# A recorded single-core trunk layer: RWKV inverses in place through one scratch tensor, scores in pieces, ACT-issued stores, new prices in the recorder

## The chip, the cores and the metric

The kernel runs on one core of one Trainium2 chip. Its time is the device time in microseconds (us) of one execution. The engines of the core are PE (matrix products into PSUM banks), DVE, ACT and POOL (elementwise work; POOL cannot read PSUM) and SP, which here only issues DMA transfers. Each engine works through its own instructions in the order in which the program holds them, and waits when an operand is not there yet.

## The reference, cut to what matters

One layer of a hybrid encoder reads 1024 prompt tokens and 64 sample tokens through one wide input projection and feeds three token mixers: RWKV-7 (A), mLSTM (B) and stick-breaking attention (C). Their outputs are gated, projected, merged and projected again. The change is in mixer A, whose state goes through the tokens one by one:

```python
def step(S, inp):
    r_t, w_t, k_t, v_t, kk_t, a_t = inp
    sa = jnp.einsum('bhvk,bhk->bhv', S, -kk_t)
    S = (S * w_t[:, :, None, :] + sa[..., None] * (kk_t * a_t)[:, :, None, :]
         + v_t[..., None] * k_t[:, :, None, :])
    return S, jnp.einsum('bhvk,bhk->bhv', S, r_t)
```

The kernel takes 64 tokens (a chunk) at a time. Inside a chunk the recurrence is a triangular system, so each chunk of each of the 8 heads needs the inverse of a 64 x 64 unit triangular matrix, before the chain over the chunks can use it.

## The kernel before, in words

**Two strands.** `main` is the strand of projections. Its 78 blocks of the input projection each take 72 products: 8 slices of the contraction, three products for each slice (high and low parts of a float32r split, lines 755 on), and three groups of 384, 384 and 320 tokens. That is 5616 products whose operands are called `xh` or `xl` and `whl`. After them come the merges (operands `heapr` and `whl` first), and then the tail (output projection, layer norm, last gates). `side` is the strand of the mixers: A for four pairs of heads, each in two halves of 8 and 9 chunks, then B for four heads, then C for four pairs of heads, and then `m_prep`, which loads, multiplies and splits the first operand of the merges. The merges wait for it (`m_begin`, and `merge` by `self.ycd`).

**What sets the order.** All work is recorded while the program is built. `Sched` keeps a clock for each engine, and every helper (`mm`, `act`, `tt`, `scan`, `dma` ...) hands it a price. After each projection product, `poll` looks at the waiting side tasks and records those whose operands are ready by these clocks. So between a side product and the one that needs its result stand as many projection products as the prices say will fill the time. When the projections run out, the side products stand alone. The profile attributes work to the helpers' lines: L321 is every product, L328 every transpose, L353 ACT, L358 and L376 DVE, L360 POOL, L427 a DMA.

**Mixer A for one half of a pair.** `a_front` loads the projected columns from DRAM and prepares them; its part "scores" makes two masked 128 x 128 matrices for each chunk (buffer `SC`) and stores the 32 x 32 diagonal blocks of the first one to the DRAM tensor `nd` with 8 DMAs. `a_inverse` loads them with one block in a partition, and inverts all blocks of the half at once on POOL, in 31 steps of two instructions, from `N` into a second buffer `Q` that begins as the identity. DVE copies a transposed form, and two DRAM tensors, `qd` and `xd`, take the results. `a_corner` loads both with 10 DMAs, then completes the 64 x 64 inverses with products of 32 x 32 on PE. `a_chain` follows the chunks with three dependent steps of PE and ACT or DVE for each chunk. Inverses follow one another on POOL; the chain of one half, the inverse of the next and the front of a third run beside each other.

**Stores.** The blocks of projections for B, C and the gates leave through four staging buffers. `store` spawns a task that issues the DMA on SP, in whose queue it waits until ACT or DVE has written the buffer.

Of the kernel before, what the change touches and what calls it, by code (L numbers as in the profile page):

```python
# [9 lines left out]
F32 = mybir.dt.float32  # L10
# [3 lines left out]
OP = mybir.AluOpType  # L14
# [10 lines left out]
HEAP = 17256  # L25
# [281 lines left out]
class K:  # L307
# [75 lines left out]

    def rsqrt(self, y, x, h, eps):
# [440 lines left out]
    def raw(self, i, col, dst, kind, done):  # L825
# [8 lines left out]
        def ev(g, t0, n, bank):  # L834
# [10 lines left out]
            self.store(i_, dst[:, t0:t0 + n], d, done if g == 2 else None)  # L845
# [4 lines left out]
    def store(self, i, out, d, done):  # L850

        self.kept |= {i}
# [457 lines left out]
    def a_all(self):  # L1310
# [5 lines left out]
        inv = [self.must(n, True) for n in (1024, 1024, 256, 288)]  # L1316
        self.bkd = self.must(1024, True)
        lists = ("Z", "ya", "bn")
        self.ast = [*Z, *cst["ya"], *cst["bn"], *[x for k, x in cst.items() if k not in lists], *inv, self.bkd]
# [12 lines left out]
    def a_front(self, p, hf):  # L1332
# [93 lines left out]
        SC = yield from self.get(nc * 256)  # L1426
        UV = yield from self.get(nc * 128)
        sc4, uv3 = SC.v(nc, 2, 128), UV.v(nc, 128)
        bd5 = self.bkd.v(2, 2, 2, 128)

# [10 lines left out]
        for c0 in range(0, nc, 4):  # L1441
            cr = range(c0, min(c0 + 4, nc))
            m = len(cr)
            bs = [(yield from self.bank()), (yield from self.bank())]
# [26 lines left out]
            for i in range(min(m, 2)):  # L1471
                w = (m + 1 - i) // 2
                yield self.act(uv3[64:128, c0 + i:c0 + m:2, :], b2[64 * i:64 * i + 64, :w * 128].rearrange(
# [738 lines left out]
```

## Time and profile before

| | |
|---|---|
| runs | 1891.88 us median of 3 (1881.05 to 1899.76) |
| profiled execution | 1887.65 us, its span 1885.9 us |
| mean granted PE clock | 0.973 of full speed |
| busy share of the span | DVE 62%, ACT 42%, POOL 30%; PE's share is with the rows below |
| DMA | mean 110 GB/s, 207338 of 212280 packets in the queue of SP |

Busy PE time counts products that overlap in the array, so a share near 100% means that PE did not run dry, and not that it was at its peak. The granted clock has two levels, 2.4 GHz (1.0) and 1.2 GHz; a stretch's value is a mean. An idle engine costs time only where PE, which has the most work, waits for it.

### The profile page before, as it was taken

To read this page: it belongs to the slowest core of one execution; us is meant where nothing else is said; L and a number is where in the kernel's file an instruction comes from. 1 tells how busy PE (TensorE), PEld (TensorE's weight loads), DVE (VectorE), ACT (ScalarE), POOL (GpSimd) and SP (SyncE) were. 2 spreads that over 40 slices of the span, in tenths; PEclk is the share of its full clock that TensorE was granted. 3 is DMA by queue.
4 is the path that set the end of the run, shared out by engine and by line. 5 is a ranking of instruction groups with operands and counts; after the bars stand their busy time and mean duration, and the time that the engine had idled before them with its cause. 6 is when DMAs were issued, how large, how long until landed. Compare 5 with 4: busy or idle time off the path is not lost.

```text
span 1885.9 us, 30250 instructions
## 1 busy us (share of the span) xinstructions
PE 1763.8 (94%) x10873; PEld 1619.1 (86%) x10873; DVE 1178.7 (62%) x2588; ACT 784.9 (42%) x1781; POOL 556.9 (30%) x1028
## 2 busy tenths in 40 slices
PE   6999999989999999999999999999966799988999
PEld 5999888979898899999999999999844799866787
DVE  8346466564647554756876266666666678888643
ACT  5444444344444344545444354645453222211321
POOL 6007445362617522810611221212020000345100
PEclk9999999999999999999999999999977899989999
DMA  4323423223232332343633442423211877522321
GB/s 148 109 83 87 112 71 95 80 83 109 77 92 67 110 85 77 99 119 114 198 122 115 141 125 68 116 90 110 72 53 35 264 229 232 158 90 78 125 80 60
DMA packets 212280, 206.55 MB, mean 110 GB/s; under 512 B 41592, under 2 KB 180650, under 8 KB 212130
## 3 DMA queue, kind: packets, MB, share of 16 engines
q1 hardware_dynamic: 207338, 191.86, 33.4%
q0 software_dynamic: 4704, 12.71, 2.1%
q8 instruction: 86, 1.41, 0.3%
q14 instruction: 64, 0.52, 0.1%
q10 hardware_dynamic: 88, 0.04, 0.0%
HBM read 136.25 MB, written 68.34 MB: 108 GB/s over the span
## 4 chain that ended last, share of the span: by engine, by line
PE 41%; issue 8%; DVE 8%; ACT 2%; POOL 2%; DMA 1%; SPq 0%; POOLq 0%; DVEq 0%; ACTq 0%
PE bk L321 39%; PE bk L328 3%; DVE heap L376 2%; DVE heap L397 2%; DVE heap L358 2%; DVE heapr L358 1%; POOL heap L414 1%; ACT heapr L353 1%; ACT heap L353 1%; DMA heap<-yz 1%; DMA heap<-gd 0%; DVE whl L358 0%; DVE heap L408 0%; POOL heap L419 0%; ACT whl L353 0%
## 5 line engine op out<-in xcount | busy, mean ns | idle before, releaser
L321 PE MATMUL bk<-xh,whl 128*128 128x384 f32 (+3 forms) x3792 | 1065.9, 342 | 0.3 <-DVE heap L376 0.3
L321 PEld LDWEIGHTS bk<-xh,whl 128*128 128x128 f32 (+1 forms) x3792 | 685.0, 188 | 11.9 <-issue 3.0
L321 PE MATMUL bk<-xl,whl 128*128 128x384 f32 (+3 forms) x2184 | 674.7, 330 | 1.7 <-POOL xl L360 1.2
L321 PEld LDWEIGHTS bk<-xl,whl 128*128 128x128 f32 (+1 forms) x2184 | 406.0, 189 | 6.0 <-POOL xl L360 1.8
L353 ACT ACTIVATE heap<-bk 64x64 f32<-64x64 f32 (+10 forms) x639 | 216.4, 346 | 433.1 <-PE bk L321 143.9
L360 POOL TENSOR_TENSOR heap<-heap 32x31 f32<-32x31 f32 (+33 forms) x514 | 347.0, 675 | 159.4 <-DMA heap<-nd 121.2
L328 PE MATMUL bk<-ident,heap 128*128 128x128 f32 (+3 forms) x942 | 184.7, 293 | 57.1 <-DVE heap L376 18.5
L358 DVE TENSOR_TENSOR whl<-heap,whl 128x1024 fp32r<-128x1024 f32 (+1 forms) x114 | 122.8, 1078 | 147.8 <-ACT whl L353 121.8
L328 PEld LDWEIGHTS bk<-ident,heap 128*128 128x128 f32 (+3 forms) x942 | 125.3, 149 | 82.3 <-DVE heap L376 21.4
L358 DVE TENSOR_TENSOR heap<-heap 128x256 f32<-128x256 f32 (+18 forms) x376 | 186.4, 501 | 13.6 <-DMA heap<-yz 2.8
L321 PE MATMUL bk<-heap,heap 128*128 128x128 f32 (+3 forms) x1360 | 170.6, 255 | 18.7 <-ACT heap L353 16.6
L321 PEld LDWEIGHTS bk<-heap,heap 128*128 128x128 f32 (+2 forms) x1360 | 142.9, 162 | 46.2 <-ACT heap L353 31.6
L353 ACT ACTIVATE heap<-bk,pc 128x384 f32<-128x384 f32 (+5 forms) x218 | 114.3, 547 | 137.4 <-PE bk L321 102.0
L321 PE MATMUL bk<-heapr 128*128 128x256 f32 (+2 forms) x524 | 131.0, 355 | 12.1 <-DVE heapr L358 5.6
L376 DVE SCALAR_TENSOR_TENSOR heap<-heap 128x4 f32<-128x4 f32 (+9 forms) x265 | 106.0, 402 | 50.4 <-ACT heap L353 45.0
L321 PE MATMUL bk<-heapr,whl 128*128 128x384 f32 (+2 forms) x648 | 119.6, 343 | 18.8 <-ACT heapr L353 18.5
L353 ACT ACTIVATE heap<-heap 64x64 f32<-64x64 f32 (+9 forms) x328 | 111.0, 343 | 61.5 <-DVE heap L376 20.1
L353 ACT ACTIVATE whl<-heap 128x1024 fp32r<-128x1024 f32 (+1 forms) x116 | 105.4, 910 | 68.0 <-PE bk L321 58.9
L321 PEld LDWEIGHTS bk<-heapr,whl 128*128 128x128 f32 x648 | 110.6, 192 | 25.2 <-ACT heapr L353 20.3
L321 PEld LDWEIGHTS bk<-heapr 128*128 128x128 f32 x524 | 89.4, 202 | 29.8 <-DVE heapr L358 12.1
L397 DVE TENSOR_TENSOR_SCAN heap<-heap,cst 128x128 f32<-128x128 f32 (+8 forms) x68 | 96.3, 1420 | 28.2 <-POOL heap L414 16.2
L353 ACT ACTIVATE heap<-bk,hb 128x384 f32<-128x384 f32 (+1 forms) x120 | 67.5, 563 | 109.5 <-PE bk L321 88.9
(153 smaller groups left out, 1808.4 us busy)
## 6 DMA issues: line engine op xcount, KB each, us to landing
heap<-in_w_in_dram SPq DMA_DIRECT2D x77, 512.0 KB
heap<-gt SPq DMA_DIRECT2D x24, 544.0 KB
gt<-heap SPq DMA_DIRECT2D x48, 192.0 KB
heap<-in_x_prompt_dram SPq DMA_DIRECT2D x16, 512.0 KB
heap<-crd SPq DMA_DIRECT2D x12, 544.0 KB
heap<-yd SPq DMA_DIRECT2D x24, 272.0 KB
heap<-yz SPq DMA_DIRECT2D x24, 272.0 KB
heap<-in_w_branch_dram SPq DMA_DIRECT2D x24, 256.0 KB
```

Source lines behind the costliest of these rows:

```text
L321: lambda: self.nc.tensor.matmul(out, lhsT, rhs, start=start, stop=stop, skip_group_check=more),
L328: lambda: self.nc.tensor.transpose(out, in_, self.ident[:p, :p]), load=(0.82 * fsize(in_), d))
L353: return self.nc.scalar.activation(out, in_, func, **kw)
L358: lambda: self.nc.vector.tensor_tensor(out=out, in0=a, in1=b, op=op))
L360: lambda: self.nc.gpsimd.tensor_tensor(out=out, in0=a, in1=b, op=op))
L376: lambda: self.nc.vector.scalar_tensor_tensor(out=out, in0=a, scalar=s, in1=b, op0=op0, op1=op1))
L397: return self.S.emit("dve", fsize(out) * 1.06 + 65, rd, [out], lambda: self.nc.vector.tensor_tensor_scan(out=out, data0=d0, data1=d1, init ...
L414: return self.S.emit("pool", fsize(out) * 1.0 + 130, [in_], [out], lambda: self.nc.gpsimd.affine_select(out=out, in_=in_, pattern=pattern, ...
```

## The change: what it does

**Prices.** A float32r product of n columns costs 13 + n/2.4 ns in the recorder, 1 + n/2.4 before (line 316). A scan on DVE costs 2.13 ns for each element and 90, before 1.06 and 65.

**Inverses.** The masked first score matrix gets its sign from a second mask (`maskb`), so the inverse adds where it subtracted, in 30 steps, in place in `N`. There is no `Q`, no `qd` and no `xd`. `nd` holds whole 64 x 64 blocks; the scores go there with one or two DMAs for every four chunks, as soon as these are made. Blocks of 32 x 32 are loaded from it, inverted and stored back to it, now by rows of 32 numbers; the corner loads 64 x 64 blocks and transposes one half of each on DVE (`tr32`).

**Scores in pieces.** `SC` and `UV` are buffers for four chunks each, freed by the chain after every four chunks.

**Stores.** The stores of the blocks for B, C, the mLSTM's output gate and the merge gates are issued by ACT, behind the ACT instruction that writes the staging buffer: 156 DMAs. Those of kind `z`, which DVE writes, and A's stay with SP.

```diff
-            c = d = 1 + (213.0 if n < 256 else n / 2.4)
+            c = d = 13 + (213.0 if n < 256 else n / 2.4)
...
+    def tr32(self, out, in_):
+
+        return self.S.emit("dve", fsize(out) * 1.06 + 65, [in_], [out], lambda: self.nc.vector.transpose(out, in_))
...
-        return self.S.emit("dve", fsize(out) * 1.06 + 65, rd, [out], lambda: self.nc.vector.tensor_tensor_scan(
+        return self.S.emit("dve", fsize(out) * 2.13 + 90, rd, [out], lambda: self.nc.vector.tensor_tensor_scan(
...
-            self.store(i_, dst[:, t0:t0 + n], d, done if g == 2 else None)
+            self.store(i_, dst[:, t0:t0 + n], d, done if g == 2 else None, kind != "z")
...
-    def store(self, i, out, d, done):
-
+    def store(self, i, out, d, done, now=False):
+
+        if now:
+            self.dma(out, d, "a")
+            if done:
+                self.have.add(done)
+            return
...
-        inv = [self.must(n, True) for n in (1024, 1024, 256, 288)]
+        inv = [self.must(n, True) for n in (1024, 240, 288)]
...
-                yield self.stt(sc4[:, c, 0, :], bs[0][:, i * 128:(i + 1) * 128], nsb[:, c:c + 1],
-                               self.mask[:, c % 2 * 64:c % 2 * 64 + 128], OP.mult, OP.mult)
+                yield self.stt(sc4[:, i, 0, :], bs[0][:, i * 128:(i + 1) * 128], nsb[:, c:c + 1],
+                               self.maskb[:, c % 2 * 64:c % 2 * 64 + 128], OP.mult, OP.mult)
             for e in range(min(m, 2)):
-                yield self.tt(sc4[:, c0 + e:c0 + m:2, 1, :],
+                yield self.dma(nd[c0 + e:c0 + m:2].rearrange("c h s j -> (h s) c j"),
+                               sc4[:, e::2, 0, 64 - 64 * e:128 - 64 * e], "s")
...
-        nd = self.dr.tile([2, 18, 32, 32], F32, name="nd", bufs=3)
-        for k in range(2):
-            for h in range(2):
-                s = slice(64 * h + 32 * k, 64 * h + 32 * k + 32)
-                for e in range(2):
-                    o = 64 - 64 * e + 32 * k
-                    yield self.dma(nd[k, h * nc + e:(h + 1) * nc:2].rearrange("c s j -> s c j"),
-                                   sc4[s, e::2, 0, o:o + 32], "s")
...
+        blk = [nd.rearrange("c h s j -> (c h) s j")[0:B, 32 * k:32 * k + 32, 32 * k:32 * k + 32] for k in range(2)]
+        rows = [N[k * B:(k + 1) * B, :1024].rearrange("p (s j) -> p s j", j=32) for k in range(2)]
         for k in range(2):
...
-        for j in range(31, 0, -1):
-            w = 32 - j
+            yield self.dma(rows[k], blk[k], "s")
+        yield self.memset(N[0:P, :1024][:, ::33], 1.0)
+        yield
+        n3 = N[0:P, :1024].rearrange("p (s j) -> p s j", j=32)
+        for j in range(30, 0, -1):
+            w = 31 - j
...
-                    q3[:, j:j + 1, j:32].to_broadcast([P, j, w]), OP.mult, IE)
-            yield self.tt(q3[:, 0:j, j:32], q3[:, 0:j, j:32], t3, OP.subtract, IE)
+                    n3[:, j:j + 1, j + 1:32].to_broadcast([P, j, w]), OP.mult, IE)
+            yield self.tt(n3[:, 0:j, j + 1:32], n3[:, 0:j, j + 1:32], t3, OP.add, IE)
...
-            yield self.dma(qd[k, 0:B].rearrange("c s j -> c (s j)"), Q[k * B:(k + 1) * B, :1024], "s")
-        yield self.dma(xd[0:B].rearrange("c s j -> c (s j)"), N[0:B, :1024], "s")
+            yield self.dma(blk[k], rows[k], "s")
...
+        for v, cs in parts:
+            yield self.tr32(x13[:, cs, :], v[:, :, 0:32])
...
+                    self.free(SC[c // 4], UV[c // 4])
```

**Where instructions move.** PE holds the same 9887 products and transposes in both programs. Their order differs from the first halves of A on. Counted in the two orders: ahead of the first product of A's fronts (its second operand is the constant `bd`) stand 396 projection products before and 357 now; ahead of the last 32 x 32 product of A's corners 3471 and 2346; between the recording of the first and last product of the eight chains of A stand 1691 projection products and 451 others before, 1295 and 610 now.

PE, where the input projections end (`xh`/`xl`, `whl`), mixer C (`heapr` alone, transposes through `ident`) and the merges (`heapr,whl`) meet. Before, the last projection product is the third row, and 168 rows of C stand between it and the first merge:

```order
L321 MATMUL bk_67<-xh,whl 128x320
L321 MATMUL bk_67<-xl,whl 128x320
L321 MATMUL bk_67<-xh,whl 128x320
L328 MATMUL bk_70<-ident,heap 128x128 x3
L321 MATMUL bk_72<-heapr 128x256 x2
L321 MATMUL bk_68<-heapr 128x256
...
L321 MATMUL bk_68<-heapr 128x256 x3
L321 MATMUL bk_72<-heapr 128x256 x4
L321 MATMUL bk_65<-heapr,whl 128x384 x12
L321 MATMUL bk_66<-heapr,whl 128x384 x12
```

Now the merges follow the last projection product at once; C's last product stands some 540 products further ahead:

```order
L321 MATMUL bk_67<-xl,whl 128x320
L321 MATMUL bk_67<-xh,whl 128x320 x2
L321 MATMUL bk_67<-xl,whl 128x320
L321 MATMUL bk_67<-xh,whl 128x320
L321 MATMUL bk_65<-heapr,whl 128x384 x12
L321 MATMUL bk_66<-heapr,whl 128x384 x12
```

All C products have moved ahead, between projections; behind this place the order of the merges is the same.

SP's queue at the second half of A, where the scores of one half are stored while the inverse of the first half comes back. Before (`nd` and `qd` in slices of 32 partitions, `xsd` the projections for A):

```order
L427 DMA nd<-heap_76 32x5x32
L427 DMA xsd<-heap 128x384
L427 DMA nd<-heap_76 32x4x32
L427 DMA nd<-heap_76 32x5x32
L743 DMA heap<-in_w_in_dram 128x8x128
L427 DMA nd<-heap_76 32x4x32
```

Now (64 x 64 pieces from all partitions, `nd<-heap 16x32x32` is the inverse going back):

```order
L431 DMA nd<-heap_76 128x2x64
L431 DMA xsd<-heap 128x384
L431 DMA nd<-heap_76 128x2x64
L431 DMA xsd<-heap 128x384
L747 DMA heap<-in_w_in_dram 128x8x128
L431 DMA nd<-heap_76 128x2x64
```

SP holds 648 instructions now, 884 before: 156 stores have gone to ACT, and each half of A has 13 of these DMAs where it had 23.

## Rows read from the trace of the kernel before

**Rows 1.** The profile's page: the span, the busy times, the busy tenths of PE in 40 slices of 47.1 us, and the granted clock in tenths.

```profile
span 1885.9 us, 30250 instructions
PE 1763.8 (94%) x10873; PEld 1619.1 (86%) x10873; DVE 1178.7 (62%) x2588; ACT 784.9 (42%) x1781; POOL 556.9 (30%) x1028
...
PE   6999999989999999999999999999966799988999
...
PEclk9999999999999999999999999999977899989999
```

**Rows 2.** Busy time of each engine by stretch. Columns: stretch, length, busy us and (records) of PE, weight loads, DVE, ACT, POOL, then granted clock, DMA share, GB/s. The stretches are the fronts and inverses of A, the rest of A with B, C beside projections, C alone with the preparation of the merges, the merges, the tail.

```profile
97.10:821.40 724.30, 697.40 (x4760) 650.81 (x4758) 412.87 (x1177) 318.73 (x834) 332.69 (x600) 0.99 0.32 91
821.40:1097.60 276.20, 273.67 (x1774) 262.98 (x1767) 172.98 (x489) 129.90 (x317) 63.28 (x129) 1.00 0.43 135
1097.60:1360.50 262.90, 256.20 (x1650) 240.40 (x1649) 179.11 (x204) 136.14 (x261) 46.70 (x152) 1.00 0.31 94
1360.50:1477.10 116.60, 69.72 (x323) 52.65 (x321) 74.19 (x91) 49.49 (x94) 13.83 (x45) 0.75 0.22 67
1477.10:1626.00 148.90, 148.88 (x883) 147.69 (x884) 112.72 (x205) 37.36 (x67) 3.37 (x6) 0.99 0.74 241
1626.00:1885.90 259.90, 236.13 (x1022) 188.08 (x1021) 169.26 (x297) 64.64 (x118) 65.17 (x36) 0.95 0.27 87
```

**Rows 3.** PE in order of time (start, length, operation, count, idle time before it and what ended that): the last projection product and the first merges.

```profile
1360.50 0.31 PE L321 MATMUL bk<-xh,whl 128*128 128x320 f32 x1
...
1451.89 0.62 PE L321 MATMUL bk<-heapr 128*128 128x256 f32 x3 [0.34 <-DVE heapr L358]
1459.30 1.77 PE L321 MATMUL bk<-heapr,whl 128*128 128x384 f32 x3 [6.79 <-ACT heapr L353]
1464.86 1.77 PE L321 MATMUL bk<-heapr,whl 128*128 128x384 f32 x3 [3.79 <-ACT heapr L353]
1470.61 1.76 PE L321 MATMUL bk<-heapr,whl 128*128 128x384 f32 x3 [3.98 <-ACT heapr L353]
1476.36 5.88 PE L321 MATMUL bk<-heapr,whl 128*128 128x384 f32 x23 [3.98 <-ACT heapr L353]
```

**Rows 4.** PE groups by line and tile in the stretch 1360.5 to 1477.1 (count after the x, busy us, mean ns of one, idle time before them).

```profile
L321 PE MATMUL bk<-heapr 128*128 128x256 f32 (+2 forms) x152 | 46.2, 406 | 10.4 <-ACT heapr L353 5.0 <-DVE heapr L358 4.1 <-DVE heap L358 0.5
L328 PE MATMUL bk<-ident,heap 128*128 128x128 f32 (+1 forms) x134 | 29.6, 343 | 17.6 <-DVE heapr L358 10.6 <-DVE heap L358 6.3 <-ACT heap L353 0.7
L321 PE MATMUL bk<-heap 128*128 128x128 f32 (+3 forms) x24 | 6.9, 379 | 0.0
L321 PE MATMUL bk<-heapr,whl 128*128 128x384 f32 x10 | 5.8, 639 | 18.8 <-ACT heapr L353 18.5
```

**Rows 5.** The same groups in 1100 to 1300, where C stands between projections.

```profile
L321 PE MATMUL bk<-xh,whl 128*128 128x384 f32 (+1 forms) x481 | 136.6, 338 | 0.0
L321 PE MATMUL bk<-xl,whl 128*128 128x384 f32 (+1 forms) x241 | 79.2, 329 | 0.0
L321 PE MATMUL bk<-heapr 128*128 128x256 f32 (+2 forms) x260 | 58.6, 328 | 0.7 <-DVE heapr L358 0.5
L328 PE MATMUL bk<-ident,heap 128*128 128x128 f32 (+1 forms) x230 | 41.0, 274 | 4.0 <-DVE heap L358 3.9
L321 PE MATMUL bk<-heap 128*128 128x128 f32 (+3 forms) x48 | 11.5, 330 | 0.0
```

**Rows 6.** The stretch 1500 to 1600 of the merges, columns as in rows 2.

```profile
1500.00:1600.00 100.00, 100.00 (x604) 100.00 (x603) 76.01 (x140) 23.57 (x42) 1.12 (x2) 1.00 0.71 232
```

**Rows 7.** PE groups of projection products in A's stretch, 97 to 821.4.

```profile
L321 PE MATMUL bk<-xh,whl 128*128 128x384 f32 (+3 forms) x2051 | 581.8, 344 | 0.0
L321 PE MATMUL bk<-xl,whl 128*128 128x384 f32 (+2 forms) x1025 | 338.2, 330 | 0.0
```

**Rows 8.** Who waited for whom (total us, times, longest us): products and weight loads of PE in 97.1 to 821.4.

```profile
PE bk L321 <- ACT heap L353: 17.6, 21, 2.2
...
PEld bk L321 <- ACT heap L353: 37.7, 64, 2.4
```

**Rows 9.** Three of the eight inverses on POOL, from first to last instruction (the first, the sixth, the last), columns as in rows 2.

```profile
146.80:188.30 41.50, 40.39 (x255) 38.89 (x254) 28.26 (x58) 18.66 (x47) 36.99 (x70) 1.00 0.23 66
...
564.50:606.50 42.00, 38.25 (x232) 34.70 (x231) 33.35 (x106) 20.06 (x56) 37.26 (x64) 0.96 0.20 60
...
741.20:794.10 52.90, 51.74 (x319) 51.08 (x319) 35.63 (x76) 25.72 (x48) 47.66 (x67) 1.00 0.30 88
```

**Rows 10.** Waits of the whole span (total us, times, longest us): POOL's for the loads of the inverses.

```profile
POOL heap L360 <- DMA heap<-nd: 121.2, 8, 24.7
```

**Rows 11.** The DMAs that ACT issues (shortest, median, longest ns), by the tile they write, and the waits of SP's queue.

```profile
L427 ACTq DMA_DIRECT2D grd<-heap x6: 246/250/271, 208.6 to 217.9; - x6
...
SPq L427 <- ACT heap L353: 583.9, 166, 11.6
```

**Rows 12.** Waits of PE in the merges and the tail, 1480 to 1886.

```profile
PE bk L328 <- DVE heap L376: 18.5, 5, 5.9
```

**Rows 13.** DMAs from POOL's queue (count, KB each, median us from issue to landing).

```profile
out_c_p_dram<-heap POOLq DMA_DIRECT2D x4, 64.0 KB, 2.2
```

More of the change, by code (lines that the diff above doesn't have):

```diff
@@ L24 @@
 COL_CQ, COL_CK, COL_CV, COL_CZ, COL_G = 4744, 5256, 5768, 6280, 6792
-HEAP = 17256
+HEAP = 17264
 SW = 12928
@@ L1315, in a_all @@
                "V2": self.must(128, True), "U2": self.must(128, True), "bn": [self.must(256, True) for _ in range(2)]}
-        inv = [self.must(n, True) for n in (1024, 1024, 256, 288)]
+        inv = [self.must(n, True) for n in (1024, 240, 288)]
         self.bkd = self.must(1024, True)
+        mb = self.must(192, True)
+        self.maskb = mb[:, :192]
+        yield self.cp(self.maskb, self.mask[:, :])
+        yield self.ts(self.maskb[:, 64:128], self.mask[:, 64:128], -1.0, OP.mult)
         lists = ("Z", "ya", "bn")
-        self.ast = [*Z, *cst["ya"], *cst["bn"], *[x for k, x in cst.items() if k not in lists], *inv, self.bkd]
+        self.ast = [*Z, *cst["ya"], *cst["bn"], *[x for k, x in cst.items() if k not in lists], *inv, self.bkd, mb]
         self.bond = self.dr.tile([4, 128, NT], F32, name="bond")
@@ L1425, in a_front @@
         self.S.note(f"   scores {p}{hf}")
-        SC = yield from self.get(nc * 256)
-        UV = yield from self.get(nc * 128)
-        sc4, uv3 = SC.v(nc, 2, 128), UV.v(nc, 128)
+        SC, UV = [], []
         bd5 = self.bkd.v(2, 2, 2, 128)
+        nd = self.dr.tile([9, 2, 64, 64], F32, name="nd", bufs=3)
         def diag(i):
@@ L1443, in a_front @@
             m = len(cr)
+            SC.append((yield from self.get(m * 256)))
+            UV.append((yield from self.get(m * 128)))
+            sc4, uv3 = SC[-1].v(m, 2, 128), UV[-1].v(m, 128)
             bs = [(yield from self.bank()), (yield from self.bank())]
@@ L1552, in a_corner @@
             for h in range(2):
-                yield self.mm(bs[h][top[h], c * 32:(c + 1) * 32], x13[low[h], c, :], sc4[low[h], c, 0, 96 - c % 2 * 64:128 - c % 2 * 64], True, True)
+                yield self.mm(bs[h][top[h], c * 32:(c + 1) * 32], x13[low[h], c, :], tri(c)[low[h], 32:64], True, True)
         for h in range(2):
-            for e in range(2):
-                yield self.act(sc4[top[h], e::2, 0, 96 - 64 * e:128 - 64 * e],
-                               bs[h][top[h], :nc * 32].rearrange("p (a b) -> p a b", b=32)[:, e::2, :], AF.Copy, scale=-1.0)
+            for v, cs in parts:
+                yield self.act(v[top[h], :, 32:64],
+                               bs[h][top[h], :nc * 32].rearrange("p (a b) -> p a b", b=32)[:, cs, :], AF.Copy)
             self.unbank(bs[h])
@@ L1599, in a_chain @@
             C0, nc_ = (0, 8) if hf == 0 else (8, 9)
-            bk3, kr3, sc4, uv3 = BK.v(nc_, 128), KR.v(nc_, 128), SC.v(nc_, 2, 128), UV.v(nc_, 128)
+            bk3, kr3 = BK.v(nc_, 128), KR.v(nc_, 128)
             for c in range(nc_):
+                sc3, uv2 = (x[c // 4].v(min(4, nc_ - c // 4 * 4), n, 128)[:, c % 4] for x, n in ((SC, 2), (UV, 1)))
+                uv2 = uv2[:, 0, :]
                 if c + C0 == 16:
@@ L1626, in a_chain @@
                 u = cb[:, 128:256]
[L1627 to L1628 removed]
+                yield self.mm(u, sc3[:, 0, :], R1[:, :], True, True)
+                yield self.ts(uv2[0:64, :], u[kr, :], -1.0, OP.mult)
                 for h in range(2):
@@ L1637, in a_chain @@
                     yield self.stt(zn[r, r], zz[r, r], PC[r, c:c + 1], ZP[r, r], OP.mult, OP.add)
-                yield self.mm(ry, sc4[:, c, 0, :], U2[:, :], False, True, more=True)
+                yield self.mm(ry, sc3[:, 0, :], U2[:, :], False, True, more=True)
                 zi ^= 1
@@ L1647, in a_chain @@
                     yb = None
-            self.free(BK, KR, PC, SC, UV)
+            self.free(BK, KR, PC)
             self.S.note(f"      chained {p}{hf}")
```

50 lines of the change are left out of this document (21 added, 29 removed).

## The prediction

> **What bounds the kernel now.** I read the page first. PE is busy for 94% of the span, yet its digits fall to 6 in three slices, the only ones after the start in which the granted clock falls below 8 [rows 1]. So the question is whether PE works through one fixed pile of products without a hole. The busy times by stretch answer it [rows 2]: from 97 to 1360 us and in the merges PE is nearly full, and one stretch, 1360.5 to 1477.1, has 69.7 us of work in 116.6 us, at a mean clock of 0.75. PE in order of time tells what happens there [rows 3]: at 1360.50 the last projection product runs, and from then on only C's last head pair and the preparation of the merges are left, with nothing to put between their steps. The first merges come in threes, each after a wait of 4 to 7 us for ACT, which waits for loads. PE is the bound in all other stretches; there the side strand costs only its own products, as long as they come when their operands are ready.
>
> **The exposed stretch, the largest term.** The order now puts 541 products, nearly all of the projections, between C's last product and the first merge. What does C's work cost when it stands between projections? In the merges 604 products take 100 us, 165.6 ns each [rows 6]; these have the same 384 and 320 columns as the projections. In 1100 to 1300, 481 + 241 = 722 projection products take 722 x 0.1656 = 119.6 us, so the 260 + 230 + 48 = 538 products of C, waits included, take the other 80.4 us: 0.150 us each [rows 5]. The exposed stretch holds 152 + 134 + 24 = 310 such products, and 13 of projections and merges (323 in all) [rows 2, 4]. At these prices it would take 310 x 0.150 + 13 x 0.166 = 48.7 us, and 116.6 - 48.7 = **67.9 us go**. Ends: its busy time at its clock, 69.72 x 0.75 = 52 us, would save 64; A's cheaper price (below), 0.128 us, would save 75. The preparation of the merges (the waits at 1459 to 1476) is hidden if it ends within the 541 products, 541 x 0.166 = 90 us; before it took from 1452 to 1477, so it fits. This needs no PE instruction to become faster: the pile is the same 9887.
>
> **A runs with less between its steps.** Of the 3076 projection products in A's stretch [rows 7], 1086 move behind it (counted in the orders, 3471 - 396 stand between the first product of A's fronts and the last of its corners before, 2346 - 357 = 1989 now). At 0.1656 us A's stretch shrinks by 180 us to 544 us, which is no gain by itself, since these products run later. The rest of the stretch, 724.3 - 3076 x 0.1656 = 214.9 us, is for 4760 - 3076 = 1684 records of A's own (0.128 us each, waits included) [rows 2, 7]. Waits are in it already: ACT held up products 21 times and weight loads 64 times, 55.3 us [rows 8]. In the chains, 204 steps of PE (4 pairs, 17 chunks, 3 steps), 1691 projections and 451 others stand between steps before, 1295 and 610 now. An other one costs 214.9 us over the 935 products that the order has for these records (the trace counts most of A's twice), 0.230 us. So a step had (1691 x 0.1656 + 451 x 0.230)/204 = 1.88 us of cover, and has 1.74. If every step used all of its cover, 204 x 0.14 = 29 us of waits come in; if none did, 0. Less than half of the steps wait now (85 events), and half is what I take: **+15**. B has the same kind of chain, but nearly no waits in its stretch, where PE is busy 273.67 of 276.20 us [rows 2]: 0.
>
> **Inverses.** The work of the 30 steps is the sum of j(31 - j), 4960 elements a partition, before 5456; at 36.99 us busy in 41.5 [rows 9] an inverse becomes some 4 us shorter, and the memset of `Q`, the copy and the extra loads go. POOL and the DMA queue are beside PE, so the direct gain is 0; the cover that hides an inverse, from its loads to its corner, is 73 to 88 us of products in the new order at the prices above, and it needs 41.5 us, a load of 15 us on the mean and 24.7 at most [rows 10] and the way back. If it fails, the DVE transposes of the corner wait for DMA, with the splits of weights queued behind them.
>
> **ACT-issued stores.** 156 DMAs at 250 ns [rows 11] are 39 us more on ACT, which is busy for 634 of the 1380 us from 97 to 1477 (four stretches summed [rows 2]); ACT has room, and each DMA stands behind the write it needs, so it waits for nothing. SP's queue loses its 583.9 us of waits for ACT [rows 11], and what stood behind them (loads for A, weights) is issued earlier. Both at 0; ends -10 and +10, an estimate, a quarter of those 39 us either way. Scan prices change only when scans are expected to end: with the first term.
>
> **Merges and tail.** The merges' PE order is unchanged: 0. In the tail three of the nine groups of transposes stand 15 to 24 products earlier. There PE waits for DVE, 18.5 us in 5 events [rows 12]; DVE needs the same time either way, and a wait that begins earlier mostly ends at the same moment. **+3**, ends 0 and 14.
>
> **Sum.** 1887.65 - 67.9 + 15 + 3 = 1837.8 by the profiled execution. That execution lies 4.2 us below the median of the three runs, so 1842 on the median's scale; I say **1840**. Own range of this case: 1887.65 - 75 - 10 = 1803 to 1887.65 - 64 + 29 + 10 + 14 = 1877.
>
> **Rival 1, slower: the inverses cannot follow.** A's half now gets 544/8 = 68 us where it had 90.5. The inverses form a loop on one buffer: load, POOL, store, next load. If that loop needs more than 68 us, PE waits for the difference eight times, and from 68 + 68/8 = 76.5 us on the whole first term is eaten. The last inverse took 52.9 us, beside the gates of B on DVE, the others 40 to 43 of own time; with the longest load wait, 24.7 us, and a store of 2.2 us as POOL's small ones took [rows 9, 10, 13], the loop is 79.8 us. Eight times 11.8 is 94 us: 1887.65 - 67.9 + 94 + 18 = **1932**. For it: DVE's 413 us in A would fill 76% of 544 us, not 57%. Against it: the sixth inverse ran beside a DVE busy for 33.35 of 42.00 us and took 42.0, and the load waits hold the time until the scores were made. The Trainium skill ("SBUF — State Buffer", "Who interferes with whom") states that a DVE instruction with two SBUF inputs and a GpSimd instruction that reads SBUF exclude each other, whichever is second waiting until the first ends. By that rule all eight inverses might go to 52.9 us; the last inverse agrees with it, the sixth does not, so DVE's busy share alone does not decide it here. Chance 8%.
>
> **Rival 2, no change: the chains and fronts wait more.** If each of the 204 steps waits as the 85 events do, 55.3/85 = 0.65 us, that is 133 us, 78 more than now: 1887.65 - 67.9 + 78 + 3 = **1901**. For it: the new price takes the hidden margin of 12 ns for each product out of every distance, and nothing adds one for ACT. Against it: fewer than half of the steps wait although all had nearly the same cover, and in B nearly none. Chance 15%.
>
> **Rival 3, faster still: the queues were the cause of waits in A.** With SP's queue free and the scans' prices right, half of the 55.3 us goes, the first term is worth 75, and the steps cost 0: 1887.65 - 75 - 28 = **1785**. Against it: PE's waits in A are for ACT, not for DMA [rows 8]. Chance 9%.
>
> **How the numbers follow.** The forecast has 68%. A change under 1% of the median (18.9 us) is about what a measurement of this kernel cannot tell from none. Faster by more than that (below 1873): the forecast and rival 3, 77%; within: rival 2, 15%; slower (above 1911): rival 1, 8%. The range 1800 to 1895 leaves out rival 1, a half of rival 2 and a half of rival 3, together 20%.
>
> **What would show it.** The slices of PE with 6 and a clock under 8 near 1400 us should be gone, and the merges should begin straight after a projection product, near 1410 us, with dense products for some 90 us before. The last 32 x 32 product should come between 620 and 670 us instead of 821. PE's waits for ACT in A should be 55 to 85 us. The forecast is wrong if POOL is busy without gaps through A while PE waits there for DVE or POOL (rival 1), or if A's waits for ACT exceed 110 us (rival 2), or if the preparation of the merges still holds up the first merges.

## The result, and the profile after

The changed kernel takes 1809.88 us (median of 4 runs, 1806.45 to 1819.05), the kernel before 1892.56 us in the same comparison: a ratio of 0.958, 95% interval 0.952 to 0.964. That is faster by 4.2%, and inside the range; the forecast was 1840. The profiled execution of the changed kernel, 1819.05 us, is the longest of its four; stage by stage I compare it with the profiled 1887.65 us of before, a difference of 68.6 us, where the two medians differ by 82.7.

The page's slices of PE no longer have the hole near 1400 us, and the granted clock stays at 9 tenths or more up to the tail [rows 1]:

```profile
span 1817.2 us, 30058 instructions
PE 1738.4 (96%) x10873; PEld 1604.2 (88%) x10873; DVE 1173.9 (65%) x2618; ACT 790.9 (44%) x1821; POOL 491.5 (27%) x1004
...
PE   6999999999899999999999999999999999878999
...
PEclk9999999999999999999999999999999999988999
```

PE in order of time, where the projections end: the last one is at 1397.37, and the merges follow without a wait, where ACT held up each group of three before [rows 3]:

```profile
1397.22 0.31 PE L321 MATMUL bk<-xl,whl 128*128 128x320 f32 x1
1397.37 0.31 PE L321 MATMUL bk<-xh,whl 128*128 128x320 f32 x1
1397.51 2.77 PE L321 MATMUL bk<-heapr,whl 128*128 128x384 f32 x15
```

Busy times by stretch, columns as in [rows 2]. The stages are cut at single products that every kernel has: A (first product of its fronts to its last 32 x 32 product), B (to C's first product), C (to the last side product ahead of the merges), the projections behind it (to the 24th merge product), the merges, the tail:

```profile
89.50:643.20 553.70, 526.93 (x3665) 473.80 (x3665) 373.92 (x1170) 268.69 (x786) 279.11 (x552) 0.98 0.32 89
643.20:938.70 295.50, 290.76 (x1891) 278.26 (x1884) 183.96 (x505) 144.42 (x346) 59.24 (x140) 1.00 0.42 132
938.70:1307.40 368.70, 368.64 (x2431) 354.44 (x2431) 254.81 (x297) 205.43 (x382) 53.56 (x205) 1.00 0.34 100
1307.40:1401.50 94.10, 94.10 (x575) 94.10 (x574) 21.27 (x26) 26.06 (x41) 1.25 (x6) 1.00 0.48 151
1401.50:1539.90 138.40, 138.40 (x843) 138.40 (x843) 106.70 (x197) 34.94 (x62) 2.20 (x4) 1.00 0.72 233
1539.90:1817.20 277.30, 245.04 (x1051) 196.28 (x1050) 177.82 (x301) 65.47 (x120) 64.86 (x37) 0.93 0.27 89
```

C and the 94 us behind it are full to the last tenth. To compare kernels that hold different numbers of projections in a stage, I count the projection products in it by their operands in the trace and take off 0.1656 us for each [rows 6]; what is left I call the stage's **rest**: the side strand's products, the waits, and time at the lower clock. For A now, 553.7 - 1989 x 0.1656 = 224.3 us. Cut at the same products, before and after:

| stage | projections before, after | rest before | rest after | change |
|---|---|---|---|---|
| A | 3075, 1989 | 215.3 | 224.3 | +9.0 |
| B | 1233, 1341 | 71.6 | 73.4 | +1.8 |
| C | 912, 1380 | 204.1 | 140.1 | -64.0 |
| behind C | 0, 549 | 28.5 | 3.2 | -25.3 |
| tail | 0, 0 | 266.2 | 277.3 | +11.1 |

With -0.9 at the start and -0.7 in the merges that is -69.0, against -68.7 in the spans (1885.9 to 1817.2). The gain lies in C and behind it; A and the tail give some of it back.

### The profile page after: what moved, and what is told of

Same layout as the page of the kernel before. It is cut to its first block, busy times and chain, and to the rows that moved or that the text cites. A ratio compares the mean times of both kernels' runs of the same rounds, so it can differ in the third digit from the quotient of the medians.

```text
span 1817.2 us, 30058 instructions
## 1 busy us (share of the span) xinstructions
PE 1738.4 (96%) x10873; PEld 1604.2 (88%) x10873; DVE 1173.9 (65%) x2618; ACT 790.9 (44%) x1821; POOL 491.5 (27%) x1004
## 4 chain that ended last, share of the span: by engine, by line
PE 76%; DVE 14%; ACT 5%; issue 2%; DMA 2%; ACTq 0%; POOL 0%; SPq 0%; DVEq 0%
PE bk L321 71%; PE bk L328 5%; DVE heap L376 5%; ACT heap L353 4%; DVE heap L358 2%; DVE heap L371 2%; DVE whl L358 1%; DVE heapr L358 1%; DMA heap<-gd 1%; ACT whl L353 1%; DMA heap<-in_x_prompt_dram 1%; DVE heap L412 0%; DVE xl L358 0%; ACTq L431 0%; DVE heap L381 0%
## 5 line engine op out<-in xcount | busy, mean ns | idle before, releaser
L360 POOL TENSOR_TENSOR heap<-heap 32x30 f32<-32x30 f32 (+16 forms) x498 | 309.9, 622 | 37.2
L328 PE MATMUL bk<-ident,heap 128*128 128x128 f32 (+3 forms) x942 | 180.5, 286 | 40.7 <-DVE heap L376 26.9
L358 DVE TENSOR_TENSOR heap<-heap 128x256 f32<-128x256 f32 (+15 forms) x363 | 175.5, 489 | 15.0 <-DMA heap<-yz 5.5
L321 PE MATMUL bk<-heap 128*128 128x128 f32 (+6 forms) x972 | 149.9, 277 | 5.8 <-ACT heap L353 4.7
L321 PE MATMUL bk<-heap,heap 128*128 128x128 f32 (+2 forms) x972 | 133.9, 263 | 16.6 <-ACT heap L353 13.2
L321 PEld LDWEIGHTS bk<-heap,heap 128*128 128x128 f32 (+1 forms) x972 | 104.8, 166 | 46.6 <-ACT heap L353 32.3
L353 ACT ACTIVATE heap<-heap 64x64 f32<-64x64 f32 (+10 forms) x328 | 111.2, 343 | 68.9 <-DVE heap L376 27.6
L321 PEld LDWEIGHTS bk<-heap 128*128 128x128 f32 (+2 forms) x972 | 111.7, 168 | 28.6 <-ACT heap L353 16.1
L376 DVE SCALAR_TENSOR_TENSOR heap<-heap 128x4 f32<-128x4 f32 (+8 forms) x261 | 100.8, 387 | 49.3 <-ACT heap L353 43.4
L353 ACT ACTIVATE heap<-bk,hb 128x384 f32<-128x384 f32 (+1 forms) x120 | 67.7, 564 | 139.8 <-PE bk L321 120.6
L321 PE MATMUL bk<-heapr 128*128 128x256 f32 (+2 forms) x524 | 119.9, 331 | 0.0
L401 DVE TENSOR_TENSOR_SCAN heap<-heap,cst 128x768 f32<-128x768 f32 (+8 forms) x68 | 96.4, 1422 | 33.6 <-POOL heap L418 19.6
```

The lines of the kernel that those rows point to most:

```text
L321: lambda: self.nc.tensor.matmul(out, lhsT, rhs, start=start, stop=stop, skip_group_check=more),
L328: lambda: self.nc.tensor.transpose(out, in_, self.ident[:p, :p]), load=(0.82 * fsize(in_), d))
L353: return self.nc.scalar.activation(out, in_, func, **kw)
L358: lambda: self.nc.vector.tensor_tensor(out=out, in0=a, in1=b, op=op))
L360: lambda: self.nc.gpsimd.tensor_tensor(out=out, in0=a, in1=b, op=op))
L376: lambda: self.nc.vector.scalar_tensor_tensor(out=out, in0=a, scalar=s, in1=b, op0=op0, op1=op1))
```

## Experiments

Twelve kernels ran, each with a profile, timed against the kernel before on the same chip; times of different kernels are compared by these ratios. The theories that the expectations number: **theory 1**, the gain comes from how much of the side strand still has projections beside it, which the inverses decide; its rivals give it to the prices, or to the queues that the stores leave. In the table "behind" counts products in the order of PE: side products behind the last projection with a minus, projections behind the last side product with a plus.

| kernel | inverses | product, scan price | ACT stores | us | ratio, 95% interval | behind | C: projections, length, rest | A, tail: rest |
|---|---|---|---|---|---|---|---|---|
| before | old | 1, 1.06 | no | 1892.56 | 1 | -298 | 912, 355.1, 204.1 | 215.3, 266.2 |
| the change | new | 13, 2.13 | yes | 1809.88 | 0.958 [0.952, 0.964] | +549 | 1380, 368.7, 140.1 | 224.3, 277.3 |
| inv_only | new | 1, 1.06 | no | 1822.35 | 0.962 [0.959, 0.966] | +474 | 1188, 358.4, 161.7 | 218.4, 267.9 |
| p_only | old | 13, 1.06 | no | 1865.29 | 0.985 [0.982, 0.988] | +159 | 1053, 355.7, 181.3 | 219.1, 275.4 |
| s_only | old | 1, 2.13 | no | 1919.56 | 1.015 [1.010, 1.020] | -484 | 864, 367.3, 224.2 | 222.1, 270.6 |
| st_only | old | 1, 1.06 | yes | 1914.41 | 1.014 [1.011, 1.017] | -437 | 750, 349.8, 225.6 | 220.3, 260.3 |
| ps | old | 13, 2.13 | no | 1882.05 | 0.994 [0.992, 0.996] | -186 | 1149, 360.6, 170.3 | 222.2, 275.4 |
| no_s | new | 13, 1.06 | yes | 1834.67 | 0.969 [0.966, 0.972] | +861 | 1212, 369.2, 168.5 | 214.3, 275.0 |
| no_st | new | 13, 2.13 | no | 1819.78 | 0.962 [0.959, 0.965] | +654 | 1359, 369.0, 143.9 | 216.0, 278.4 |
| no_p | new | 1, 2.13 | yes | 1793.31 | 0.948 [0.944, 0.952] | +120 | 1533, 393.8, 139.9 | 206.5, 271.5 |
| p7 | new | 7, 2.13 | yes | 1800.73 | 0.953 [0.950, 0.956] | +438 | 1389, 368.6, 138.6 | 212.5, 274.6 |
| p30 | new | 30, 2.13 | yes | 1881.22 | 0.994 [0.992, 0.996] | +972 | 1257, 368.4, 160.2 | 242.9, 281.0 |
| inv_s | new | 1, 2.13 | no | 1784.74 | 0.944 [0.941, 0.948] | +186 | 1539, 393.9, 139.1 | 206.7, 272.7 |
| res_off_pool | new, last gates off POOL | 1, 2.13 | yes | 1759.97 | 0.932 [0.929, 0.935] | +120 | 1533, 393.1, 139.2 | 205.7, 233.2 |

### One part alone

**inv_only**: the kernel after, with both prices and the stores as before.

```diff
-            c = d = 13 + (213.0 if n < 256 else n / 2.4)
+            c = d = 1 + (213.0 if n < 256 else n / 2.4)
...
-        return self.S.emit("dve", fsize(out) * 2.13 + 90, rd, [out], lambda: self.nc.vector.tensor_tensor_scan(
+        return self.S.emit("dve", fsize(out) * 1.06 + 65, rd, [out], lambda: self.nc.vector.tensor_tensor_scan(
...
-            self.store(i_, dst[:, t0:t0 + n], d, done if g == 2 else None, kind != "z")
+            self.store(i_, dst[:, t0:t0 + n], d, done if g == 2 else None)
```

> The kernel of the change with the old prices of products and scans and the stores back on SP: only the in-place inverses, the one scratch tensor and the scores in pieces are left. In its order no side product stands behind the last projection product (298 before), and 474 projection products stand behind the last side product (549 with the whole change). Theory 1 (what counts is that no side work is left alone when the projections end; about 0.23 us for each of the 298 products, 68 us): 1892 - 68 = about 1825, ratio 0.965. Theory 2 (SP's queue, freed of the stores' waits, made the side strand faster): nothing of that is here, so about as before, over 1875. Theory 3 (the prices did it, by better distances between steps): the old prices are here, so over 1875 too.

Measured 1822.35 us, as theory 1 has it: the inverses and the pieces alone give 70 us. A needs 2175 projections where it took 3075, and those 900 stand in B, C and behind C. The inverses start every 65 us (eight, from 142.1 to 595.8), where they started every 85 (146.8 to 741.2). One lasts 39.5 us on the mean from its first instruction to its last, 44.8 before, so most of the difference lies between the inverses. POOL's waits for their loads are a part of it, 121.2 us before [rows 10]:

```profile
POOL heap L423 <- DMA heap<-nd: 64.9, 7, 18.5
```

Which of the edits to the inverses does it (fewer steps, fewer DMAs, scores stored in pieces as they are made, smaller buffers) was not taken apart.

**p_only**: the kernel before with the new price of a product (first hunk above, the other way round).

> The kernel before with only the price of a float32r product changed from 1 to 13 ns and n/2.4. No side product stands behind the last projection product, and 159 projection products (26 us) cover the preparation of the merges, which took some 25 us after C's last product before. Theory 1: as with the inverses alone, about 1825 (ratio 0.965), up to 10 us more where those 26 us do not cover all. Theory 2: about as before. Theory 3: about as the whole change, 1810.

Measured 1865.29 us, a miss by 40 us. The exposed stretch is gone here too, by the order (159 projections behind the last side product) and by the page (no slice of PE under 8 between the first and the tail), and yet only 1.5% came of it: C with 1053 projections has a rest of 181.3 us. That the last side product has projections behind it is thus not enough; C also needs them beside it, and A still uses up 2931 here (2175 in inv_only), with 159 more behind C.

**s_only**, **st_only** and **ps**: the kernel before with the scan price, with the ACT-issued stores, and with both new prices.

```diff
-        return self.S.emit("dve", fsize(out) * 1.06 + 65, rd, [out], lambda: self.nc.vector.tensor_tensor_scan(
+        return self.S.emit("dve", fsize(out) * 2.13 + 90, rd, [out], lambda: self.nc.vector.tensor_tensor_scan(
```

> The kernel before with only the scan price changed. 484 side products stand behind the last projection product, 298 before. Theory 1: 186 more exposed products at 0.23 us are 43 us lost, some 12 us of waits in C won back: about 1920, ratio 1.015, and PE's hole before the merges longer by some 45 us. If right distances alone gain: under 1885.

> The kernel before with nothing changed but the issue of 156 stores by ACT. In its order of PE 437 side products stand behind the last projection product, 298 before. Theory 1 (what counts is how much of the side work is left without projections): those 139 more, at the exposed price of the stretch before, 116.6 us for 323 records or 0.36 us, less the 0.13 us that they cost between projections, are 32 us, so 1915 to 1930. Theory 2 (the stores themselves free SP's queue and so remove waits in A): faster than before, 1880 or less. Theory 3 (the stores cost ACT's time): like theory 1 on the whole, but with PE's waits for ACT in A above the 55.3 us of before by 15 us or more.

> The kernel before with both new prices and nothing else. 186 side products stand behind the last projection product (298 before, none with the product price alone). Theory 1: 186 x 0.23 = 43 us stay exposed of some 68, so 25 us gain, and the scan price takes away most of the 41 us that the run with the product price alone spent waiting in C beyond the densest run: about 1850, ratio 0.977, near the 1865 of that run. If exposed products did not matter and only the distances of steps did: as the whole change without its inverses, 1825 or less.

s_only took 1919.56 us, a hit; st_only 1914.41 us, just under the span of theory 1 and far from the rival. With the old inverses either part makes the kernel slower, since A and B use up more projections (3108 and 1248 in s_only, 3192 and 1278 in st_only, 3075 and 1233 before), and 484 or 437 side products are left alone. ACT's own work for the DMAs does not show in A, where theory 3 looked for it: PE and its weight loads wait less for ACT there than before (47.7 us in place of 55.3 [rows 8]):

```profile
PEld bk L321 <- ACT heap L353: 32.2, 59, 2.4
...
PE bk L321 <- ACT heap L353: 15.5, 20, 2.1
```

ps, 1882.05 us, missed its 1850: 186 side products are still alone, and B's rest (83.0 us) and the tail's are larger than before.

### The change less one part

**no_s**, **no_st** and **no_p**: the kernel after with the old scan price, the old stores, the old price of a product (one hunk of inv_only each).

> The whole change with the old scan prices. Nothing is exposed (861 projection products behind the last side product). Theory 1 with its second term (the price of scans takes some 17 us of C's waits away): 1810 + 17 = about 1827, with PE waiting for DVE in C's stretch as before. If C's waits went for another reason (SP's queue, or more projections beside C): 1810.

> The whole change with the stores back on SP. Nothing is exposed (654 projection products behind the last side product). Theory 1: as the whole change, 1810 within 10 us. Theory 2: most of the gain is lost, 1850 or more.

> The whole change with the old price of a product. Nothing is exposed, 120 projection products (20 us) stand behind the last side product, 549 with the whole change; the other 429 stand between side steps of A, B and C instead. Theory 1 (a projection product is worth something only where it covers a wait): 1810 or up to 15 us less, with PE waiting less for ACT in A, and up to 5 us lost in front of the merges. Theory 3 (the right price of a product is what gains): well over the whole change, 1840 or more.

no_s took 1834.67 us, by the ratios 21 us more than the change; its C has a rest of 168.5 us, and PE waits there for DVE, where the changed kernel has no wait of PE in all of C. The waits of PE in C of no_s:

```profile
PE bk L328 <- DVE heap L358: 9.0, 11, 2.5
PE bk L321 <- DVE heapr L358: 6.3, 11, 1.4
PE bk L328 <- DVE heapr L358: 1.8, 4, 0.6
```

C's scans run on the same engine, and the old price was half of what they take: 1.06 x 1024 + 65 is 1150 ns, the new one 2.13 x 1024 + 90 is 2271 ns. Groups of scans in C, in the kernel before:

```profile
L397 DVE TENSOR_TENSOR_SCAN heap<-heap,cst 128x1024 f32<-128x1024 f32 x8 | 18.2, 2277 | 0.0
L397 DVE TENSOR_TENSOR_SCAN heap<-heap,cst 128x896 f32<-128x896 f32 x8 | 16.2, 2022 | 6.6 <-POOL heap L414 6.6
L397 DVE TENSOR_TENSOR_SCAN heap<-heap,cst 128x768 f32<-128x768 f32 x8 | 14.0, 1752 | 4.5 <-POOL heap L419 4.5
```

no_st took 1819.78 us; its interval overlaps that of the change. **no_p took 1793.31 us and beats the change**: inside the whole change the new price of a product costs some 18 us, where theory 1 had up to 15. (The two intervals just touch, 0.952. The same pair without the ACT-issued stores, inv_s below and no_st, leaves no doubt of the order: 0.944 [0.941, 0.948] with the old price, 0.962 [0.959, 0.965] with the new.) The theory that this price was part of the gain falls, though with the old inverses it gained 1.5% (p_only).

**p7**, **p30**: the kernel after with 7 or 30 in place of 13.

> The whole change with 30 ns in the place of 13. 972 projection products stand behind the last side product, 549 with 13. Theory 1: 423 more projections are taken out from between side steps and cover nothing where they go: waits of 20 to 50 us come in, in A and C: 1830 to 1860. If an earlier side strand is good in itself: 1810 or less.

> The whole change with 7 ns in the price of a product, between 1 (1793.3 us) and 13 (1809.9 us); 30 gave 1881. Theory 1 (each projection product that the price takes out from between dependent steps costs cover, in proportion): 438 projection products stand behind the last side product, 120 and 549 at the two ends, so 1800 to 1810, nearer to the upper end. Theory 2 (the trace's own overhead, some 10 ns a product, is the best price, so that 7 lies near a minimum and 13 only a little past it): below 1793.

1, 7, 13, 30 give 1793.31, 1800.73, 1809.88, 1881.22 us. 7 shows no sign of a minimum, though its interval overlaps those of both neighbours. By the ratios a ns costs some 1.5 us from 1 to 13 and 4.0 us from 13 to 30. The last is more than theory 1 had, 1830 to 1860. With 30, 972 projections have gone behind the last side product and are missing between the steps of A (rest 242.9 us), B (91.0 us) and C (160.2 us). PE's waits for ACT in A of p30, 76.5 us:

```profile
PE bk L321 <- ACT heap L353: 24.8, 45, 2.2
...
PEld bk L321 <- ACT heap L353: 51.7, 93, 2.5
```

The theory that an earlier side strand is always better falls with it.

**inv_s**: inverses and scan price alone, product price and stores as before.

> The inverses, the scores in pieces and the scan price, without the ACT-issued stores and with the old price of a product. 186 projection products stand behind the last side product (120 with the ACT-issued stores). Theory 1 (the stores matter only through the order, 10 us either way): 1785 to 1803. Theory 2 (the ACT-issued stores are worth more than 10 us once C is filled well): above 1803.

Measured 1784.74 us. Against inv_only (0.962 [0.959, 0.966]) the scan price is worth 1.8% (0.944 [0.941, 0.948]); against no_p the ACT-issued stores are worth nothing that these runs can tell, the intervals overlap.

### C in one view

Busy times in C, columns as in [rows 2], of inv_only, no_s and no_p, one fence each:

```profile
973.80:1332.20 358.40, 345.15 (x2239) 323.64 (x2238) 247.82 (x285) 193.45 (x363) 61.60 (x202) 1.00 0.31 93
```

```profile
905.40:1274.60 369.20, 351.12 (x2263) 326.57 (x2262) 253.70 (x300) 201.10 (x378) 60.52 (x202) 1.00 0.31 93
```

```profile
960.40:1354.20 393.80, 392.67 (x2583) 379.82 (x2583) 253.22 (x290) 208.50 (x382) 69.38 (x207) 1.00 0.32 97
```

In eleven of the fourteen kernels C lasts 350 to 369 us, with anything from 750 to 1389 projections in it, and no engine but PE is near full (DVE 254.81 of 368.70 us in the changed kernel). PE is full from 1380 projections on (368.64 of 368.70 us in the changed kernel), and with 1533 or 1539 C lasts 394 us: 153 projections more, 25.1 us more, 0.164 us each. With fewer, PE has idle time in C (13.3 us in inv_only, 18.1 in no_s), and a projection taken out of C shortens it by little and is paid for elsewhere: st_only has 162 fewer than before, 26.8 us of them at 0.1656 us, and its C is 5.3 us shorter. What makes up the 350 to 369 us where PE is not full (the chain of DVE, POOL and ACT steps for each head pair is the candidate) was not taken apart.

### The tail

In no_p, the tail lasts 271.5 us and PE waits in it for DVE. Busy times of its tail, and PE's longest wait there, as [rows 12] before:

```profile
1526.10:1797.60 271.50, 243.25 (x1052) 194.59 (x1050) 177.85 (x304) 65.81 (x120) 64.93 (x37) 0.94 0.26 88
```

```profile
PE bk L328 <- DVE heap L376: 22.9, 6, 6.1
```

DVE in order of time shows instructions on one element per partition of 0.16 us, and some of microseconds; beside the latter POOL works on 128 x 1024 tensors. Both in order of time (the second POOL row is the later of the two instructions of the first):

```profile
1599.89 2.36 DVE L358 TENSOR_TENSOR heap<-heap 128x1 f32<-128x1 f32 x1
...
1599.51 5.14 POOL L360 TENSOR_TENSOR heap<-heap 128x1024 f32<-128x1024 f32 x2
...
1602.17 0.68 DVE L358 TENSOR_TENSOR heap<-bk,heap 128x512 f32<-128x512 f32 x1
...
1602.31 2.34 POOL L360 TENSOR_TENSOR heap<-heap 128x1024 f32<-128x1024 f32 x1
...
1613.35 0.16 DVE L358 TENSOR_TENSOR heap<-heap 128x1 f32<-128x1 f32 x1
```

**res_off_pool**: no_p, with that work of POOL done by ACT and DVE. The lines are in `res`, in the last gates.

```diff
-            yield self.ts(b, b, self.rs0[:m, t:t + 1], OP.mult, nmr[:m, t:t + 1], OP.add, e="g")
-            yield self.tt(b, b, r3[:m, 0, :], OP.mult, "g")
-            yield self.tt(b, b, r3[:m, 1, :], OP.add, "g")
+            yield self.act(b, b, AF.Identity, bias=nmr[:m, t:t + 1], scale=self.rs0[:m, t:t + 1])
+            yield self.tt(b, b, r3[:m, 0, :], OP.mult)
+            yield self.tt(b, b, r3[:m, 1, :], OP.add)
```

> The whole change with the old price of a product (1793.3 us before), and in the last gates two 128 x 1024 tensor-tensor instructions of each of the nine groups moved from POOL to DVE, the one with two per-partition scalars from POOL to ACT. The work is the same. Theory A (DVE instructions with operands in SBUF stand still while POOL works on a 128 x 1024 tensor: one-element instructions took 2.4 to 5.8 us there instead of 0.16): DVE loses 9 x 2 instructions of 128 x 1024 to do but no longer stands still, the tail becomes 10 us or more shorter, 1770 to 1788, and one-element DVE instructions in it take under 0.3 us. Theory B (the long times are an effect of the record, or DVE's own work sets the tail): same or slower, 1793 to 1812.

Measured **1759.97 us**, beyond theory A's span, and the fastest of all: 7% under the kernel before, and by the ratios 30 us under no_p. (The 5.8 us in theory A is a row of two instructions, one of them of 128 x 1024; the longest one-element instruction took 2.36 us.) By the profiles the tail is 38 us shorter, and no wait of PE for DVE is left in it. DVE is busy for 19 us less although it does 22 us of work more (16 instructions of 1217 ns and 2 of 64 partitions). The tail of res_off_pool, and some of DVE's groups in it, then the same groups in no_p:

```profile
1524.60:1757.80 233.20, 228.82 (x1052) 185.62 (x1050) 158.88 (x322) 75.60 (x129) 5.39 (x10) 1.00 0.31 102
```

```profile
L358 DVE TENSOR_TENSOR heap<-bk,heap 128x512 f32<-128x512 f32 x31 | 21.2, 683 | 10.7 <-ACT heap L353 10.5
...
L358 DVE TENSOR_TENSOR heap<-heap 128x1024 f32<-128x1024 f32 x16 | 19.5, 1217 | 5.9 <-ACT heap L353 5.8
L358 DVE TENSOR_TENSOR heapr<-heap,heapr 128x512 fp32r<-128x512 f32 x24 | 16.4, 686 | 6.6 <-ACT heapr L353 6.5
...
L376 DVE SCALAR_TENSOR_TENSOR heap<-heap 128x1 f32<-128x1 f32 x48 | 7.5, 156 | 0.9
```

```profile
L358 DVE TENSOR_TENSOR heapr<-heap,heapr 128x512 fp32r<-128x512 f32 x24 | 27.7, 1163 | 14.1 <-ACT heapr L353 14.1
...
L358 DVE TENSOR_TENSOR heap<-bk,heap 128x512 f32<-128x512 f32 x31 | 21.2, 683 | 18.7 <-ACT heap L353 18.5
...
L376 DVE SCALAR_TENSOR_TENSOR heap<-heap 128x1 f32<-128x1 f32 x48 | 16.5, 344 | 1.5
```

The groups that became faster have both inputs in SBUF (the core's on-chip memory beside PSUM), and fell to as little as half; the group with one input in PSUM (`bk`) takes 683 ns in both; its instruction at 1602.17 above took 0.68 us beside POOL. (The splits `xl<-heap,xh`, both inputs in SBUF, took 686 and 684 ns: not each such group had run beside POOL.) Of the 38 us, 14.4 are PE's own busy time (243.25 to 228.82), which goes with the granted clock of the tail, 0.94 to 1.00. How much a shorter path of the gates adds beside the end of the contention was not told apart.

## Why the prediction was right, and where its terms were off

**Direction and place: right; the size fell short.** The exposed stretch went, by the steps that were named: no slices of 6 near 1400, merges straight behind a projection (forecast near 1410, measured 1397.5), dense products for 94 us ahead of them (90), the preparation of the merges hidden.

**The first term was too small.** The sum was -49.9 us by the profiled execution; -68.6 came (-82.7 by the medians), and this term is the reason. I took C's products at 0.150 us, from a stretch of before in which PE was full but for 4.7 us of waits [rows 5]. They take 139.8/1050 = 0.133 us now. Groups of products in C (938.8 to 1307.5) after the change, 922 + 460 projections at 0.1656 us leave 139.8 us for the other three:

```profile
L321 PE MATMUL bk<-xh,whl 128*128 128x384 f32 (+1 forms) x922 | 260.2, 336 | 0.0
L321 PE MATMUL bk<-xl,whl 128*128 128x384 f32 (+1 forms) x460 | 150.2, 327 | 0.0
L321 PE MATMUL bk<-heapr 128*128 128x256 f32 (+2 forms) x512 | 116.8, 330 | 0.0
L328 PE MATMUL bk<-ident,heap 128*128 128x128 f32 (+1 forms) x442 | 77.0, 272 | 0.1
L321 PE MATMUL bk<-heap 128*128 128x128 f32 (+3 forms) x96 | 23.2, 334 | 0.0
```

C and what lay exposed behind it gave 89.3 us (the table of stages), not 67.9. The step that failed is the 0.150 us, taken as fixed and for the 310 exposed products alone: 0.017 us less for each of all 1050 is some 18 of the 21.4 us that are missing. With it failed the sentence "Scan prices change only when scans are expected to end: with the first term", which has no price in the sum. In inv_only, with the old scan price, the rest of C is 161.7/1049 = 0.154 us a product, near the 0.150 that I took; with the right price (inv_s) it is 0.133. The rest goes with the number of projections that the recorder puts beside C, 1188 in inv_only, 1380 in the change and 1539 in inv_s: p30 has the right scan price but 1257 of them, and a rest of 160.2 us again. Beside the new inverses the scan price was a part of its own, 1.8% or 33 us from inv_only to inv_s, by the rests 23 of them in C and 12 in A.

**A: the sign came, the mechanism is not shown.** +15 was forecast, as waits of the chains' steps; +9.0 was measured. PE's waits for ACT are 57.3 us, inside the 55 to 85 that were named, but only 2.0 us above before:

```profile
PE bk L321 <- ACT heap L353: 15.6, 31, 1.4
```

```profile
PEld bk L321 <- ACT heap L353: 41.7, 95, 1.6
```

The events are more (126, before 85) and shorter. PE's idle time in A has not grown: 553.70 - 526.93 = 26.8 us, before 724.30 - 697.40 = 26.9 [rows 2]. So the +9.0 shows as busy time of PE and not as idle time, and that it came near +15 is luck, at least in part. Less cover does become waits further on: in p30, with 1845 projections in A, PE is idle there for 40.4 us, in no_p, with 2142, for 20.5. Besides, the loss is no property of the new inverses: with the old price of a product (no_p) A's rest is 206.5 us, under the 215.3 of before. I charged the loss to the number of projections left between steps, without asking which edit took them out. Part of the 224.3 us may belong to this one execution, whose clock in A was 0.98: no_st has 216.0 us at the same prices, at a clock of 1.00.

**B**, taken at 0, has +1.8. **The last corner** came at 643 us, inside 620 to 670.

**Rival 1 did not come.** The inverses take 36 to 41 us each; the first, the fifth and the last, columns as in [rows 9]:

```profile
130.60:168.30 37.70, 35.87 (x221) 34.68 (x221) 23.34 (x49) 16.45 (x41) 33.39 (x69) 0.95 0.31 89
393.40:429.60 36.20, 33.17 (x278) 29.81 (x277) 23.92 (x66) 19.37 (x63) 31.66 (x63) 1.00 0.25 72
575.30:616.00 40.70, 39.61 (x300) 35.75 (x299) 25.20 (x99) 17.44 (x60) 34.61 (x67) 1.00 0.23 68
```

None went to 52.9 us. The rule from the Trainium skill ("SBUF — State Buffer", "Who interferes with whom") that I weighed there describes the tail: two SBUF inputs on DVE and a GpSimd instruction that reads SBUF exclude each other. The trace agrees: the one-element instruction that began at 1599.89 ended within 0.03 us of the first of the two POOL instructions, and the one with an input in PSUM at 1602.17 was not held up. In A the same shows in little: DVE's tensor-tensor instructions of 128 x 256 with both inputs in SBUF, between 130.6 and 616.0 us, take 420 ns on the mean without POOL beside them and 585 with it. Half of POOL's steps in the inverses last 0.56 us or less; its tensor-tensors of 128 x 1024 in the gates take 2.6 us on the mean.

**Rival 2 did not come** with the price at 13, but its argument, that the price takes the hidden margin out of every distance between steps, is what the four prices show: at 30 it has eaten nearly all of the gain. **Rival 3** did not come either. inv_s and no_p come near its 1785 us, but with the old price of a product, by C (rests of 139.1 and 139.9 us) and A (206.7 and 206.5), while SP's queue gave nothing: in inv_s it still has the stores.

**Stores: 0 was right** within what runs can tell. SP's waits for ACT fell from 583.9 us [rows 11] to 63.7, and nothing came of it. PE hardly waited for a DMA (1.5 us in the whole span now), and the queue was not free either: its two longest waits for DVE rose from 672.6 us to 983.6. Before, then now:

```profile
SPq L427 <- DVE heap L358: 375.7, 84, 13.0
SPq L427 <- DVE heap L376: 296.9, 93, 18.7
```

```profile
SPq L431 <- DVE heap L376: 510.5, 110, 23.1
SPq L431 <- DVE heap L358: 473.1, 85, 17.1
...
SPq L431 <- ACT heap L353: 63.7, 18, 12.5
```

**The tail** was taken at +3, ends 0 and 14; measured +11.1. PE's wait there is the one that I named [rows 12], longer by half. Behind it stands POOL, which a list of PE's waits does not name: with the gates' work off POOL the wait is gone (res_off_pool), and the 48 one-element instructions of L376 take 470 ns on the mean here, 350 before. Why more of them meet POOL now was not taken apart:

```profile
PE bk L328 <- DVE heap L376: 26.9, 8, 6.1
```

## What to carry to other kernels

Where one strand of products fills the gaps of another, count the fillers in each stage: a filler in a stage whose own steps set its length is free, one behind the last such step earns nothing. So a price in a list scheduler has to be right for the slow dependent instructions (here the scans, a factor of two), though here that paid only with the new inverses: with the old ones it cost 1.5%. A true overhead added to the filler's price takes margin away, and is to be timed at several values before it is kept. When an engine waits for tiny instructions of another, see what a third one runs at that moment.

## What was not expected of the hardware

A DVE instruction on one element per partition, 0.16 us by itself, took 2.36 us beside a 128 x 1024 tensor-tensor on POOL, and the 24 splits of 128 x 512 took 1163 ns on the mean, 686 ns with POOL idle. With 22 us more of its own work DVE was busy for less time in that stretch, 158.88 us in place of 177.85, once POOL stood still.
